# A two-block transformer in float32r: early blocks of the feed-forward corrected one by one, their products held back, and single weight blocks placed 32 bytes into their tiles

## The chip, the cores and the metric

The kernel runs on one core of a Trainium2 chip. The metric is the device time of one execution in microseconds (us), from several runs, of which the median is given. The engines are named as the profile names them: PE (TensorE, with PEld for its weight loads), DVE (VectorE), ACT (ScalarE), POOL (GpSimd) and SP (SyncE, whose queue carries the weight transfers).

## The reference

The first block has two layers (latent attention, gated linear attention, neighbourhood attention, a merge and a SwiGLU); its output of 256 tokens by 1024 goes through a second block of two layers. Each layer of the second block is

```python
x = layer_norm(ALPHA * x + 0.5 * swiglu_2(x, ffn1_w_in[l], ffn1_w_out[l]), ln_g[l, 0], ln_b[l, 0])
mix = hybrid_mixer(x, ...)
x = layer_norm(ALPHA * x + mix, ln_g[l, 1], ln_b[l, 1])
x = layer_norm(ALPHA * x + 0.5 * swiglu_2(x, ffn2_w_in[l], ffn2_w_out[l]), ln_g[l, 2], ln_b[l, 2])

def swiglu_2(x, w_in, w_out):
    h = x @ w_in
    gate, up = h[..., :D_FF], h[..., D_FF:]
    return (jax.nn.silu(gate) * up) @ w_out
```

with D = 1024 and D_FF = 2816, all in float32. The first block's layers end in the same SwiGLU behind an RMS norm.

## The kernel before

**Products.** Activations lie transposed: features on the partitions, tokens along the free dimension, so that a feature block is 128 by T. Layer 0 of the first block has T = 512, everything behind it T = 256. Each product is made of three matmuls in float32r (`mm3`, L261 to L265): weights and activations are split into a high and a low part, and high by high, high by low and low by high are added up in PSUM. A weight block of 1024 columns is loaded on SP's queue into `raw`, ACT makes `whi` of it (L250), DVE subtracts to `wlo` (L251). Both lie in tiles of 1088 columns, from column 0 or, where the product has T = 256, from column 32. There are four buffers of each; every fifth block uses a second pool, `wx`.

**Feed-forward.** `ffn_in` makes 44 blocks of 128 columns, gate and up of each of 22 pairs in turn (24 matmuls of 256 columns for a block at T = 256). `cb` takes a pair and makes one tile `u`: tanh on ACT (L1535), two operations on DVE (L1536, L1538), and a split on ACT and DVE (L495, L496). `ffn_out` makes 8 blocks of 66 matmuls over the 22 tiles `u`. A feed-forward at T = 256 stands in five places: in layer 1 of the first block (F1 in what follows), and twice in each layer of the second block (F2 and F3, F4 and F5).

**Early blocks.** PE doesn't wait for the norm ahead of a feed-forward. The blocks before `e.n` runs out (16 in these five places) are multiplied with the scaled but not yet normalized activations, `xg`, and corrected afterwards (`early_steps`, L329). The first `e.kout` of them (four, two in the first block) go through together, in banks of the PSUM pool `pa` (tag `at`, five banks); the norm's sums run through PE in between (`e.stats`). The others take a bank each of the pool `pp` (tag `mm`, three banks). Where a layer norm or a shift comes before, the moving operand has 258 columns; the two more give the terms of the correction. Weights of early blocks with 258 columns lie from column 0 of their tiles, those with 256 from column 32.

**Correction.** As soon as more than two blocks are pending, `settle` takes two, corrects both into one `fix` tile (two buffers) and hands them to `cb` at once. `fix` behind a layer norm (L1735) is a copy of two columns on DVE (`fixc`, L1738), a correction term on ACT (`lnc`, L1740), a multiplication on DVE that frees the bank (L1741), and an addition on POOL (L1742). Behind the RMS norms (L1512) it is one operation on DVE and, in layer 1 of the first block, two small ones on DVE and ACT. The normalization itself runs beside it, one of eight blocks per step (`e.apply`: L1724 on ACT, L1726 on DVE, L1728 on POOL, and a split).

**Order.** The program is traced in this order, and a planner sorts the instructions of each engine by priority and by its own estimates of time, where the data allow; each engine then runs its list strictly in order. So a setup such as `rope2` (rotary tables, masks; written behind layer 1's `ffn_in`) can be put far ahead of its place when its tiles are free.

Of the kernel before, what the change touches and what calls it, by code (L numbers as in the profile page):

```python
# [10 lines left out]
F32 = mybir.dt.float32  # L11
# [193 lines left out]
class Kern:  # L205
# [33 lines left out]

    def chunk(self, spec, T=512):  # L240


        nc = self.nc
        self.side_step()
        raw, nk, ncol, n = self.raw_chunk(spec)
        o = 32 if T == 256 else 0
        hi, lo = (self.wlast.tile([128, 1088], F32R, tag=tag, name=self.name(tag),
                                  bufs=4 if self.wlast is self.wp else 1)[:, o:o + 1024] for tag in ("whi", "wlo"))
        self.pad(self.wlast, 16)
        nc.scalar.copy(hi[:, :n], raw[:, :n])  # L250
# [3 lines left out]
    def units(self, specs, T=512):  # L254
# [11 lines left out]

    def gproj(self, spec_lists, xs, t0, t1, cb, kout=0, tail=False, early=None, ready=None, pre=()):

# [5 lines left out]
        per = 512 // T  # L274
        todo, i, got, first = list(spec_lists), 0, list(pre), bool(kout)
        if early is not None:
            i, got = yield from self.early_steps(early, todo, cb, per, T)
            first = False
            if todo or got:
                for _ in early.apply:  # L280
                    pass
                xs = early.xs
        while todo or got:
# [3 lines left out]
            while todo and len(got) < want:  # L287
                got += self.units(todo.pop(0), T)
            grp, got = got[:want], got[want:]
# [30 lines left out]
            if todo and not got and (first or AHEAD):  # L320
                got += self.units(todo.pop(0), T)
            for ps, us, i0 in banks:
# [5 lines left out]

    def early_steps(self, e, todo, cb, per, T):  # L329

# [7 lines left out]
        def matmuls(w, banks, k, pin=False):  # L338
            for wi, xi in ((0, 0), (1, 0), (0, 1)):
                for s in range(H):  # L340
                    m = nc.tensor.matmul(banks[s][:, :e.cols], lhsT=w[k][wi], rhs=e.x[k][:, xi, s, :e.cols],  # L341
                                         start=k == 0 and wi == 0 and xi == 0, stop=k == len(w) - 1 and xi == 1)
                    if pin:
                        self.tc.keep_in_program_order(m)

        def settle():
            nonlocal done
            n = min(per, len(pend))
            z = self.t(self.fixp, [128, 2, 256], F32, "fix")
            zr = z.rearrange("p a t -> p (a t)")  # L350
# [7 lines left out]
        if e.kout:  # L358
            while todo and len(got) < e.kout:
                got += self.units(todo.pop(0), Te)  # L360
            grp, got = got[:e.kout], got[e.kout:]
# [14 lines left out]
        while e.n > 0 and (got or todo):  # L376
            if not got:
                got = self.units(todo.pop(0), Te)
# [7 lines left out]
            if not got and todo and EAHEAD:  # L386
                got = self.units(todo.pop(0), Te if e.n > 0 else T)
            if len(pend) > per:
                settle()
# [1133 lines left out]
    def ffn_in(self, wname, l, xs, T, early=None, then=None):  # L1523

        nc = self.nc
        us = []
        parts = []

        def cb(ps, i, n):
            parts.extend(ps[:, a, :] for a in range(n))  # L1530
            while len(parts) >= 2:
                gate, up = parts.pop(0), parts.pop(0)
                u = self.t(self.fp, [128, 2, T], F32R, f"u{len(us)}")
                t = self.t(self.fp, [128, T], F32, "ft")
                nc.scalar.activation(t[:, :T], gate, AF.Tanh, scale=0.5)  # L1535
                nc.vector.scalar_tensor_tensor(out=t[:, :T], in0=t[:, :T], scalar=1.0, in1=gate, op0=ALU.add,  # L1536
                                               op1=ALU.mult)
                nc.vector.tensor_tensor(out=t[:, :T], in0=t[:, :T], in1=up, op=ALU.mult)  # L1538
                self.split(u[:, 0, :], u[:, 1, :], t[:, :T])
                us.append(u)  # L1540
# [45 lines left out]
    def rope2(self):  # L1586
        nc, cp = self.nc, self.cp
        with self.tc.tile_pool(name="r2", bufs=1) as rp:
            pos = self.t(rp, [128, 256], I32, "pos")
            nc.scalar.dma_start(out=pos, in_=self.ins["positions_2"].to_broadcast([128, 256]))  # L1590
            ang = self.t(rp, [128, 256], F32, "ang")
            nc.vector.tensor_copy(ang, pos)
            nc.vector.tensor_scalar(out=ang, in0=ang, scalar1=self.con("inv"), scalar2=None, op0=ALU.mult)
            n = self.t(rp, [128, 256], F32, "angn")
            big = 1.5 * 2.0 ** 23
# [49 lines left out]
    def ln_residual(self, scale, l, j, last=False):  # L1645
# [90 lines left out]
        def fix(ps, s, out):  # L1736
# [229 lines left out]
    def run(self):  # L1966
        nc, tc, ctx = self.nc, self.tc, self.ctx
        self.setup()
        with ExitStack() as hp:
            self.hp = hp  # L1970
            with self.pool("xp1", side="right") as self.xp, self.pool("wp1", 3, side="right") as self.wp:
                self.fixp = self.sp
# [94 lines left out]
```

## Time and profile before

| | |
|---|---|
| median of 3 runs | 2635.95 us (2635.83 to 2638.78) |
| the profiled execution's own time | 2630.1 us |
| its span, first to last instruction | 2628.3 us |
| mean granted TensorE clock | 0.991 |
| PE busy | 2522.5 us (96%), 17510 matmuls |
| DVE busy | 1867.1 us (71%) |
| ACT busy | 1308.2 us (50%) |
| POOL busy | 292.1 us (11%) |
| moved by DMA | 381.23 MB, mean 145 GB/s |

The profile is of one execution. Shares are averages over stages with different limits; ends of matmuls are modelled, so a busy PE isn't one at its peak, and the count of matmuls in a stretch says more than its busy time. PEclk is the granted clock as a share of 2.4 GHz. Where an engine stood idle, the view says which instruction's end let it go on.

### The profile page before, as it was taken

The numbers are of one execution on the slowest core, as the hardware profiler recorded it, in microseconds if no ns is written. First come the engines' busy times: TensorE is split into PE (matmuls) and PEld (weight loads), VectorE is DVE, ScalarE is ACT, GpSimd is POOL, SyncE is SP. The second block draws the span as 40 slices with busy tenths as digits, with TensorE's granted clock in tenths as the row PEclk, the third lists the DMA queues.
The fourth block names the chain that finished last, engine by engine and source line by source line (L and its number), as shares of the span: only waits on it lengthen the run. The fifth ranks groups of instructions, "written<-read, shape, count | busy, mean of one in ns | idle before, by whom it ended". The sixth has DMA issues, their size and how long they took to land. (4 is left out here: it accounts for less than half of the span.)

```text
span 2628.3 us, 44800 instructions
## 1 busy us (share of the span) xinstructions
PE 2522.5 (96%) x17510; PEld 2229.6 (85%) x17510; DVE 1867.1 (71%) x3318; ACT 1308.2 (50%) x2307; POOL 292.1 (11%) x368
## 2 busy tenths in 40 slices
PE   7989999999999999899999999999989999999998
PEld 4867778778777778788999999998789999977897
DVE  6677576756887865665788657667797686678965
ACT  5466633324432223566447545446475565565643
POOL 0021000110000001010020000003040040031301
PEclk9999999999999999999999999999999999999999
DMA  6332144332455543231446655553346646632563
GB/s 246 108 91 83 52 137 152 105 120 89 153 181 164 182 152 103 89 93 60 158 145 195 193 182 189 189 181 121 109 133 210 195 153 202 196 109 88 179 194 119
DMA packets 122451, 381.23 MB, mean 145 GB/s; under 512 B 25216, under 2 KB 28160, under 8 KB 122240
## 3 DMA queue, kind: packets, MB, share of 16 engines
q1 hardware_dynamic: 118784, 373.51, 45.2%
q10 hardware_dynamic: 3456, 4.86, 0.6%
q8 instruction: 138, 2.26, 0.4%
q14 instruction: 73, 0.60, 0.1%
HBM read 377.27 MB, written 1.05 MB: 144 GB/s over the span
## 5 line engine op out<-in xcount | busy, mean ns | idle before, releaser
L251 DVE TENSOR_TENSOR wlo<-raw,whi 128x1024 fp32r<-128x1024 f32 (+1 forms) x628 | 766.3, 1223 | 441.4 <-ACT whi L250 425.5
L250 ACT CAST whi<-raw 128x1024 fp32r<-128x1024 f32 (+1 forms) x628 | 637.7, 1018 | 826.2 <-PE mm L264 538.2
L263 PE MATMUL mm<-x,whi 128*128 128x256 f32 (+1 forms) x2410 | 764.8, 318 | 2.8 <-ACT whi L250 1.7
L264 PE MATMUL mm<-x,whi 128*128 128x256 f32 (+1 forms) x2410 | 760.6, 316 | 0.1
L265 PE MATMUL mm<-x,wlo 128*128 128x256 f32 (+1 forms) x2410 | 760.3, 316 | 0.1
L263 PEld LDWEIGHTS mm<-x,whi 128*128 128x128 f32 x2410 | 453.0, 188 | 48.6 <-issue 9.8
L265 PEld LDWEIGHTS mm<-x,wlo 128*128 128x128 f32 x2410 | 454.8, 189 | 33.6 <-issue 1.7
L264 PEld LDWEIGHTS mm<-x,whi 128*128 128x128 f32 x2410 | 454.9, 189 | 33.2 <-issue 1.7
L263 PE MATMUL mm<-u,whi 128*128 128x256 f32 (+1 forms) x1056 | 314.0, 297 | 0.0
L264 PE MATMUL mm<-u,whi 128*128 128x256 f32 (+1 forms) x1056 | 313.9, 297 | 0.0
L265 PE MATMUL mm<-u,wlo 128*128 128x256 f32 (+1 forms) x1056 | 313.3, 297 | 0.0
L341 PE MATMUL mm<-xg,whi 128*128 128x258 f32 (+1 forms) x1120 | 207.6, 286 | 16.4 <-DVE fixc L1738 7.2
L649 DVE SCALAR_TENSOR_TENSOR fix<-raw,csil,fix 128x512 f32<-128x512 f32 x280 | 199.0, 756 | 14.6 <-DMA raw<-in_ws_dram 14.4
L263 PEld LDWEIGHTS mm<-u,whi 128*128 128x128 f32 x1056 | 198.2, 188 | 10.7 <-issue 2.5
L265 PEld LDWEIGHTS mm<-u,wlo 128*128 128x128 f32 x1056 | 199.0, 188 | 7.2
L264 PEld LDWEIGHTS mm<-u,whi 128*128 128x128 f32 x1056 | 199.0, 188 | 6.7
L341 PEld LDWEIGHTS mm<-xg,whi 128*128 128x128 f32 x1120 | 177.1, 193 | 18.9 <-ACT whi L250 7.9
L341 PE MATMUL mm<-xg,wlo 128*128 128x258 f32 (+1 forms) x560 | 159.5, 285 | 0.0
L341 PEld LDWEIGHTS mm<-xg,wlo 128*128 128x128 f32 x560 | 108.2, 193 | 0.0
L732 ACT ACTIVATE P<-at,nmx 128x256 f32<-128x256 f32 (+1 forms) x160 | 88.5, 559 | 24.3 <-DVE nmx L727 21.5
L263 PE MATMUL mm<-whi,x 128*128 128x256 f32 x320 | 92.1, 288 | 6.9 <-ACT v L419 4.3
L725 DVE TENSOR_REDUCE mx<-at 128x1 f32<-128x512 f32 (+1 forms) x112 | 75.2, 686 | 32.0 <-PE at L954 13.0
(395 smaller groups left out, 3922.4 us busy)
## 6 DMA issues: line engine op xcount, KB each, us to landing
raw<-in_ws_dram SPq DMA_DIRECT2D x648, 512.0 KB, 3.5
raw<-in_ws_dram SPq DMA_DIRECT2D x56, 384.0 KB, 3.4
PT<-in_ws_dram SPq DMA_DIRECT2D x8, 512.0 KB, 6.8
h<-in_h_dram ACTq DMA_DIRECT2D x8, 256.0 KB, 3.8
nm<-in_na_rpb_dram SPq DMA_DIRECT2D x16, 96.0 KB, 6.6
braw<-in_na_rpb_dram SPq DMA_DIRECT2D x16, 96.0 KB, 6.5
nv<-in_h_dram ACTq DMA_DIRECT2D x4, 256.0 KB, 6.1
v<-in_h_dram ACTq DMA_DIRECT2D x4, 256.0 KB, 8.0
```

The costliest lines, as they stand in the source:

```text
L250: nc.scalar.copy(hi[:, :n], raw[:, :n])
L251: nc.vector.tensor_tensor(out=lo[:, :n], in0=raw[:, :n], in1=hi[:, :n].bitcast(F32), op=ALU.subtract)
L263: nc.tensor.matmul(out, lhsT=a[0], rhs=b[0], start=start, stop=False)
L264: nc.tensor.matmul(out, lhsT=a[0], rhs=b[1], start=False, stop=False)
L265: nc.tensor.matmul(out, lhsT=a[1], rhs=b[0], start=False, stop=stop)
L341: m = nc.tensor.matmul(banks[s][:, :e.cols], lhsT=w[k][wi], rhs=e.x[k][:, xi, s, :e.cols], start=k == 0 and wi == 0 and xi == 0, stop=k == ...
L649: nc.vector.scalar_tensor_tensor(out=acc[s], in0=w[:, j, :], scalar=x, in1=acc[s], op0=ALU.mult, op1=ALU.add)
L725: nc.vector.tensor_reduce(out=mx, in_=ps, axis=AX.X, op=ALU.max)
L732: nc.scalar.activation(P[:, i, :], ps[:, i, :], AF.Exp, bias=nm[:, i:i + 1], scale=scale, accum_out=sm[:, i:i + 1])
```

## The change

Six things change. In the feed-forward at T = 256, `settle` takes one block at a time as soon as more than one is pending, corrects it with `e.fix` into half of a `fix` tile, and puts the pair into a list `held`. A held pair is multiplied (`unit`) when its buffer is wanted again, or one by one behind the pairs of the main loop. There are four `fix` buffers in the second block (two, as before, in the first). Early blocks with an odd number take their bank from `pa` in place of `pp`. The addition in `fix` behind a layer norm goes from POOL to DVE, in the mixers too. And the first weight chunk of blocks 6, 18 and 23 of `ffn_in` and of block 0 of `ffn_out` lies from column 8 of its tiles (32 bytes), if it is loaded for T = 256. To make room, `rope2`'s tables use `ft` tiles of the feed-forward's pool instead of a pool of their own, and a pad of 32 bytes goes from the pool `yp`, into which `ls` comes.

```diff
-    def chunk(self, spec, T=512):
+    def chunk(self, spec, T=512, place=None):
...
-        o = 32 if T == 256 else 0
+        o = place if place is not None else 32 if T == 256 else 0
...
-        parts = [(self.chunk(s, T), len(s[2])) for s in specs]
+        parts = [(self.chunk(s, T, None if i else place), len(s[2])) for i, s in enumerate(specs)]
...
+        def load(to=T):
+            spec = todo.pop(0)
+            return self.units(spec, to, places.get(total - len(todo) - 1) if to == 256 else None)
...
+        dst = getattr(e, "dst", None)
+
         def settle():
             nonlocal done
+            if dst is not None:
+                e.fix(pend.pop(0)[0], 0, dst(done))
+                done += 1
+                return
             n = min(per, len(pend))
-            z = self.t(self.fixp, [128, 2, 256], F32, "fix")
+            z = self.fixtile()
...
-            banks = [self.t(self.pp, [128, 512], F32, "mm") for _ in range(H)]
+            pool, tag = (self.pa, "at") if dst is not None and i % 2 else (self.pp, "mm")
+            banks = [self.t(pool, [128, 512], F32, tag) for _ in range(H)]
...
-            if len(pend) > per:
+            while len(pend) > (per if dst is None else 1):
                 settle()
...
+    def fixtile(self):
+        return self.fixp.tile([128, 2, 256], F32, tag="fix", name=self.name("fix"), bufs=self.nfix)
...
+        us = [None] * NJ
+        parts, held = [], []
+
+        def unit(j, gate, up):
+            u = us[j] = self.t(self.fp, [128, 2, T], F32R, f"u{j}")
+            t = self.t(self.fp, [128, T], F32, "ft")
+            nc.scalar.activation(t[:, :T], gate, AF.Tanh, scale=0.5)
+            nc.vector.scalar_tensor_tensor(out=t[:, :T], in0=t[:, :T], scalar=1.0, in1=gate, op0=ALU.add,
+                                           op1=ALU.mult)
+            nc.vector.tensor_tensor(out=t[:, :T], in0=t[:, :T], in1=up, op=ALU.mult)
+            self.split(u[:, 0, :], u[:, 1, :], t[:, :T])
+
+        def release():
+            j, z = held.pop(0)
+            unit(j, z[:, 0, :], z[:, 1, :])
+
+        def dst(b):
+
+            if b % 2 == 0:
+                while len(held) >= self.nfix:
+                    release()
+                held.append((b // 2, self.fixtile()))
+            return held[-1][1][:, b % 2, :]
 
         def cb(ps, i, n):
-            parts.extend(ps[:, a, :] for a in range(n))
+            parts.extend((i + a, ps[:, a, :]) for a in range(n))
             while len(parts) >= 2:
...
+                (j, gate), (_, up) = parts.pop(0), parts.pop(0)
+                unit(j // 2, gate, up)
+            if held:
+                release()
+
+        if early is not None and T == 256:
+            early.dst = dst
...
-                           early=early)
+                           early=early, places={b: 8 for b in (6, 18, 23)})
...
-        self.proj([_colblock(wname, l, NJ, _rng(o * 128)) for o in range(8)], us, 0, T, cb, tail=True)
+        self.proj([_colblock(wname, l, NJ, _rng(o * 128)) for o in range(8)], us, 0, T, cb, tail=True,
+                  places={0: 8})
...
-        self.pad(self.yp, 8)
...
-        self.fixp = self.yp
+        self.fixp, self.nfix = self.yp, 4
...
-            pos = self.t(rp, [128, 256], I32, "pos")
+            pos = self.t(self.fp, [128, 256], F32, "ft").bitcast(I32)
...
-            ls = self.t(rp, [128, 2, 2], F32, "ls")
+            ls = self.t(self.yp, [128, 2, 2], F32, "ls")
...
-            nc.gpsimd.tensor_tensor(out=out, in0=out, in1=ck, op=ALU.add)
+            nc.vector.tensor_tensor(out=out, in0=out, in1=ck, op=ALU.add)
```

## Rows read from the trace of the kernel before

**Rows 1.** The page: busy time, share of the span, instructions of each engine.

```profile
span 2628.3 us, 44800 instructions
PE 2522.5 (96%) x17510; PEld 2229.6 (85%) x17510; DVE 1867.1 (71%) x3318; ACT 1308.2 (50%) x2307; POOL 292.1 (11%) x368
```

**Rows 2.** Stage table (PE, PEld, DVE, ACT, POOL busy; PEclk; DMA; GB/s): F3, F4, F5, F1, F2.

```profile
1929.00:1969.00 40.00, 34.71 (x276) 34.19 (x275) 39.27 (x68) 28.96 (x53) 23.07 (x22) 0.96 0.41 139
2118.00:2159.00 41.00, 35.96 (x288) 35.60 (x288) 37.91 (x67) 29.16 (x53) 20.97 (x21) 0.96 0.48 154
2439.00:2478.00 39.00, 32.96 (x272) 32.25 (x271) 37.15 (x68) 28.48 (x53) 20.33 (x21) 1.00 0.42 135
1424.00:1457.00 33.00, 33.00 (x281) 33.00 (x280) 30.73 (x71) 23.85 (x44) 0.00 (x0) 1.00 0.63 198
1613.00:1644.00 31.00, 31.00 (x266) 31.00 (x265) 27.67 (x50) 17.67 (x28) 1.86 (x4) 1.00 0.62 202
```

**Rows 3.** Waits of PE (us in total, times, longest): F3; F4; F5.

```profile
PE mm L341 <- DVE fixc L1738: 3.5, 2, 1.7
...
PE mm L341 <- DVE fix L1741: 5.0, 2, 2.9
...
PE mm L341 <- DVE fixc L1738: 3.8, 2, 2.0
```

**Rows 4.** Chain of waits through F3's early stretch, 1929 to 1969 us, shares.

```profile
by line: DVE wlo L251 23.9%; DVE x L496 11.9%; DMA raw<-in_ws_dram 10.7%; issue 10.7%; DVE fix L1741 7.7%; DVE ft L1536 7.4%; DVE ft L1538 6.4%; POOL fix L1742 5.2%; DVE u L496 4.4%; POOL h L1728 4.3%; DVE lnt L1726 4.2%; DVE fixc L1738 1.6
```

**Rows 5.** Table by stage, PE alone, 70 us of the main loops of F1 to F4.

```profile
1460.00:1530.00 70.00, 70.00 (x596) 1.00 0.59 187
1650.00:1720.00 70.00, 70.00 (x596) 1.00 0.57 185
1970.00:2040.00 70.00, 69.95 (x617) 1.00 0.67 209
2162.00:2232.00 70.00, 70.00 (x620) 1.00 0.64 198
```

**Rows 6.** The same, 50 us of the output blocks (`ffn_out`) of F1 and F5.

```profile
1540.00:1590.00 50.00, 50.00 (x427) 1.00 0.61 192
...
2560.00:2610.00 50.00, 50.00 (x444) 1.00 0.49 145
```

**Rows 7.** Groups of DVE, 1926 to 1969 us (busy us, mean ns | idle).

```profile
L251 DVE TENSOR_TENSOR wlo<-raw,whi 128x1024 fp32r<-128x1024 f32 x12 | 17.6, 1474 | 0.4 <-ACT whi L250 0.4
L1536 DVE SCALAR_TENSOR_TENSOR ft<-ft,fix 128x256 f32<-128x256 f32 x7 | 5.6, 798 | 0.0
...
L1741 DVE TENSOR_TENSOR fix<-mm,rr 128x256 f32<-128x256 f32 x10 | 4.1, 411 | 0.0
```

**Rows 8.** Groups of POOL in the same window.

```profile
L1742 POOL TENSOR_TENSOR fix<-fix,lnc 128x256 f32<-128x256 f32 x14 | 16.6, 1196 | 26.0 <-ACT lnc L1740 14.0 <-DVE fix L1741 8.9 <-DVE fixc L1738 2.0
L1728 POOL TENSOR_TENSOR h<-lnt,lnc 128x256 f32<-128x256 f32 x8 | 7.5, 939 | 2.3 <-ACT lnc L1724 1.3 <-DVE lnt L1726 0.9
```

**Rows 9.** Groups of DVE in F1's early stretch, 1424 to 1457 us.

```profile
L251 DVE TENSOR_TENSOR wlo<-raw,whi 128x1024 fp32r<-128x1024 f32 x13 | 15.9, 1220 | 2.0 <-ACT whi L250 2.0
...
L1536 DVE SCALAR_TENSOR_TENSOR ft<-ft,fix 128x256 f32<-128x256 f32 x7 | 2.9, 419 | 0.0
```

**Rows 10.** Table by stage, DVE alone, first 22 us of F5's main loop.

```profile
2480.00:2502.00 22.00, 18.50 (x27) 1.00 0.79 247
```

**Rows 11.** Timeline, F3: DVE's first corrections; ACT ahead of them.

```profile
1927.21 0.75 DVE L1741 TENSOR_TENSOR fix<-at,rr 128x256 f32<-128x256 f32 x2
...
1926.38 2.00 ACT L250 CAST whi<-raw 128x1024 fp32r<-128x1024 f32 x2 [2.15 <-DMA raw<-in_ws_dram]
1928.29 1.08 ACT L1740 ACTIVATE lnc<-rr,fixc 128x256 f32<-128x256 f32 x2
```

**Rows 12.** A wait of PE in the first mixer of the second block.

```profile
PE at L1754 <- ACT rraw L1752: 2.7, 2, 2.4
```

**Rows 13.** Timeline of ACT: a step of `rope2`.

```profile
1389.94 0.42 ACT L1642 ACTIVATE sin<-ang 128x256 f32<-128x256 f32 x1
```

More of the change, by code (lines that the diff above doesn't have):

```diff
@@ L252, in chunk, with units @@
         return (hi[:, :n].rearrange("p (k c) -> p k c", k=nk), lo[:, :n].rearrange("p (k c) -> p k c", k=nk))
-    def units(self, specs, T=512):
-        parts = [(self.chunk(s, T), len(s[2])) for s in specs]
+    def units(self, specs, T=512, place=None):
+        parts = [(self.chunk(s, T, None if i else place), len(s[2])) for i, s in enumerate(specs)]
         ncb = len(specs[0][3]) // 128
@@ L265, in mm3, with gproj @@
         nc.tensor.matmul(out, lhsT=a[1], rhs=b[0], start=False, stop=stop)
-    def gproj(self, spec_lists, xs, t0, t1, cb, kout=0, tail=False, early=None, ready=None, pre=()):
+    def gproj(self, spec_lists, xs, t0, t1, cb, kout=0, tail=False, early=None, ready=None, pre=(), places=None):
         nc = self.nc
@@ L275, in gproj @@
         todo, i, got, first = list(spec_lists), 0, list(pre), bool(kout)
+        total, places = len(todo), places or {}
+        def load(to=T):
+            spec = todo.pop(0)
+            return self.units(spec, to, places.get(total - len(todo) - 1) if to == 256 else None)
         if early is not None:
-            i, got = yield from self.early_steps(early, todo, cb, per, T)
+            i, got = yield from self.early_steps(early, todo, cb, per, T, load)
             first = False
@@ L287, in gproj @@
             while todo and len(got) < want:
-                got += self.units(todo.pop(0), T)
+                got += load()
             grp, got = got[:want], got[want:]
@@ L320, in gproj @@
             if todo and not got and (first or AHEAD):
-                got += self.units(todo.pop(0), T)
+                got += load()
             for ps, us, i0 in banks:
@@ L327, in gproj, with early_steps @@
             yield
-    def early_steps(self, e, todo, cb, per, T):
+    def early_steps(self, e, todo, cb, per, T, load):
         nc = self.nc
@@ L359, in early_steps @@
             while todo and len(got) < e.kout:
-                got += self.units(todo.pop(0), Te)
+                got += load(Te)
             grp, got = got[:e.kout], got[e.kout:]
@@ L377, in early_steps @@
             if not got:
-                got = self.units(todo.pop(0), Te)
+                got = load(Te)
             w = got.pop(0)
-            banks = [self.t(self.pp, [128, 512], F32, "mm") for _ in range(H)]
+            pool, tag = (self.pa, "at") if dst is not None and i % 2 else (self.pp, "mm")
+            banks = [self.t(pool, [128, 512], F32, tag) for _ in range(H)]
             for k in range(len(w)):
@@ L386, in early_steps @@
             if not got and todo and EAHEAD:
-                got = self.units(todo.pop(0), Te if e.n > 0 else T)
-            if len(pend) > per:
+                got = load(Te if e.n > 0 else T)
+            while len(pend) > (per if dst is None else 1):
                 settle()
@@ L1525, in ffn_in @@
         nc = self.nc
-        us = []
-        parts = []
+        us = [None] * NJ
[17 more added lines that the diff above has]
+            return held[-1][1][:, b % 2, :]
         def cb(ps, i, n):
-            parts.extend(ps[:, a, :] for a in range(n))
+            parts.extend((i + a, ps[:, a, :]) for a in range(n))
             while len(parts) >= 2:
[L1532 to L1540, printed above, removed]
+                (j, gate), (_, up) = parts.pop(0), parts.pop(0)
[4 more added lines that the diff above has]
+            early.dst = dst
         cols = [_rng(a + j * 128) for j in range(NJ) for a in (0, DFF)]
         steps = self.gproj([_colblock(wname, l, KB, c) for c in cols], xs, 0, T, cb, kout=2 if T == 512 else 4,
-                           early=early)
+                           early=early, places={b: 8 for b in (6, 18, 23)})
         if then is not None:
@@ L1587, in rope2 @@
         nc, cp = self.nc, self.cp
-        with self.tc.tile_pool(name="r2", bufs=1) as rp:
-            pos = self.t(rp, [128, 256], I32, "pos")
+        if True:
+            pos = self.t(self.fp, [128, 256], F32, "ft").bitcast(I32)
             nc.scalar.dma_start(out=pos, in_=self.ins["positions_2"].to_broadcast([128, 256]))
-            ang = self.t(rp, [128, 256], F32, "ang")
+            ang = self.t(self.fp, [128, 256], F32, "ft")
             nc.vector.tensor_copy(ang, pos)
             nc.vector.tensor_scalar(out=ang, in0=ang, scalar1=self.con("inv"), scalar2=None, op0=ALU.mult)
-            n = self.t(rp, [128, 256], F32, "angn")
+            n = self.t(self.fp, [128, 256], F32, "ft")
             big = 1.5 * 2.0 ** 23
@@ L1971, in run @@
             with self.pool("xp1", side="right") as self.xp, self.pool("wp1", 3, side="right") as self.wp:
-                self.fixp = self.sp
+                self.fixp, self.nfix = self.sp, 2
                 first = self.layer(0, 512, self.first_norm, lambda: self.load_h(hp.enter_context(self.pool("hp"))))
```

## The prediction

> **What bounds the kernel now.** I read the page first: the span is 2628.3 us, PE is busy for 2522.5 us of it, DVE for 1867.1, ACT for 1308.2, POOL for 292.1 [rows 1]. So the time can fall only where PE stands idle or runs slower than it can, and I looked for such places in the stages that the diff touches. These are five passes of `ffn_in` and `ffn_out` at T=256; I call them F1 (first block, layer 1), F2 and F3 (second block, layer 0), F4 and F5 (second block, layer 1). Each begins with an early stretch of 16 blocks (columns of 128, 24 matmuls each), whose banks are corrected afterwards, and goes on with 28 blocks and the 8 output blocks.
>
> Next I took the table by stage over the early stretches [rows 2]. In F3, F4 and F5 PE is busy for 34.71 of 40, 35.96 of 41 and 32.96 of 39 us: 5.3, 5.0 and 6.0 us idle. In F1 and F2 it is idle for nothing. The granted clock is 0.96 in the windows of F3 and F4, that is, it lay at 1.2 instead of 2.4 GHz for a part after PE had stood: 4% of 40 and 41 us, 1.6 us each. The rest ran at 1.00.
>
> Who ends the idle time says the view of waits [rows 3]: nearly all of it is PE at L341 waiting for `fix` or `fixc` on DVE, the readers that give a bank back. The chain of F3's stretch shows DVE at each step, `wlo` alone with 23.9% [rows 4]. DVE is busy for 39.27 of 40 us there [rows 2]: in this stretch it is the bound, not PE.
>
> Last I took the rate of PE where nothing stalls it. Over 70 us of the main loop PE starts 596 matmuls in F1 and F2, but 617 and 620 in F3 and F4, with the same tiles and the granted clock at 1.00 [rows 5]: 70/593 = 118.0 ns against 70/617 = 113.4 ns from start to start (three at the edges taken off). The output blocks show the same two levels, 427 in 50 us of F1, 444 of F5 [rows 6], and each pass keeps the level of its main loop. A level, once taken, holds over a whole stage, and F2's early stretch of 256 columns lies on the slow one too (266 in 31 us [rows 2]). The early stretches of 258 columns run at about 118.7 ns in F1 [rows 2], yet the main loops behind them go to 113.4 in three cases of four.
>
> **The change part by part.** The time before is the median 2635.95 us; the profiled run took 2630.1, its span 2628.3. I make the sum as a difference within the span and take it off the median.
>
> 1. The add of `fix` from POOL to DVE. In F3's window of 43 us, POOL runs 14 of these (1196 ns each, 16.6 us) beside 8 of L1728 (7.5 us) [rows 8]. DVE's own operations are stretched beside them: `wlo` takes 1474 ns, the first operation on `ft` 798 [rows 7], in F1's stretch, where POOL is idle, 1220 and 419 [rows 9]. At such prices [rows 7, 9], with 0.45 for `lnt` and 0.15 for `fixc`, F3's DVE work would be 12 x 1.22 + 14 x 0.41 + 12 x 0.15 + 8 x 0.45 + 8 x 0.42 + 19 x 0.42 + 0.4 = 37.6 us (`wlo`, `fix`, `fixc`, `lnt`, `x`, units, `rr`); the eleven groups of that window, from `wlo` with 17.6, sum to 47.3. So 9.7 us are stretch; by POOL's time 69% of it, 6.7 us, goes with the 14 adds, and 3.0 stays with L1728. The adds cost DVE 14 x 0.41 = 5.7 us.
>
> 2. Gates and ups kept. Four pairs stay in `fix` tiles until the main loop, so that the window holds 4 units, not 19/3 = 6.3: 2.3 x 3 x 0.42 = 2.9 us less. Sum for DVE: 37.6 + 5.7 - 2.9 = 40.4; adjoining operations overlap by some 0.08 us (in F1's stretch the twelve groups, from `wlo` with 15.9, sum to 36.5, while the engine is busy for 30.73 with 71 instructions [rows 2, 9]), for 80 of them 6.4. 40.4 - 6.4 + 3.0 = 37.0 us of DVE. Without idle time and low clock PE would need 43 - 5.3 - 1.6 = 36.1. DVE and PE then match, and with five more banks in turn PE can run ahead of DVE by several blocks, now by three. I leave 1.5 us of idle time in each of F3 to F5: 16.3 - 4.5 = 11.8 us gained, and the low clock with it, 2 x 1.6 = 3.2 us. Together 15.0; the bounds are 0 and 19.5, and if DVE has to wait, below zero (second rival). F1 and F2 have no stall to lose; DVE at 30.73 of 33 us leaves them cover. The four held units come to the main loop at 4 x 3 x 0.42 = 5.0 us of DVE over eight blocks. It is busy 18.50 of 22 us there in F5 [rows 10], so 23.5 less twelve overlaps of 0.08, 22.5, would fill it: hidden if its `wlo` come ahead, as in F1's 93%; if not, 1.5 us per pass, 7.5 at most.
>
> 3. More banks: the odd early blocks take `at` banks. Five are there, four hold the first blocks and one the statistics, so block 5 needs the first one back. In F3 its `fix` starts at 1927.21 [rows 11], one block of 2.85 us and more before block 5 could start. I cost it at nothing, and up to 1 us per pass if that order is lost.
>
> 4. The 32 bytes. The diff shifts one weight block at three places of F1, F3, F4 and F5 and at four of F2 (block 6 is loaded for 256 columns there): 16 blocks of 24 matmuls. Taken as a thing of its own it can cost 16 x 24 x 4.6 ns = 1.8 us if each such block falls to the slow level. But it also disturbs the rhythm of loads and matmuls. F1 and F2 from block 18 on have 1152 + 1584 matmuls at the slow level; at the fast one they gain 2736 x 4.6 ns = 12.6 us. No shift of this kind is in the trace; the bounds are -12.6 us and, if F3 to F5 fall to the slow level, +3 x 1152 x 4.6 ns = +15.9. The nearest rows are the steps from 258 to 256 columns, where the operands move as well and no stall lies between: three of four went to the fast level. So I take the gain, less 1 us for the blocks themselves: 11.6 us.
>
> The Trainium skill speaks against this term. "SBUF — State Buffer", section "SBUF: two separate sides", says that on the engine side only the port pair that VectorE and GpSimd share causes contention, and that PE never waits there. By it the start of a weight tile is nothing to PE, and the sum would be without the 11.6 us. This case's trace has two levels for one shape [rows 5], which the rule doesn't explain.
>
> 5. The rest. The mixers get the add on DVE alone (their settling stays in twos): PE waits for `rraw` there for 2.7 us in the first of the two [rows 12], behind `fix`. I take 1 us of gain for both, bounds -3 and +3. The tables of `rope2` move: `sin` is made at 1389.94 us [rows 13], before F1 begins; with `ft` tiles of F1 it can't start before F1's last units, and falls into `ffn_out`. A dozen operations of DVE and ACT of some 0.4 us stand there beside a PE that is never starved [rows 6]: nothing; at most 1.5 us, if they come ahead of a `whi`.
>
> Sum: -15.0 - 11.6 - 1.0 = -27.6 us; 2635.95 - 27.6 = 2608.
>
> **The rivals.**
> - The shift does nothing to the levels: 2635.95 - 16.0 = 2620. For it: both levels live through 28 blocks and many tile buffers without a change [rows 5, 6]; against it, the step that came with 256 columns. It is what the Trainium skill's page "SBUF — State Buffer" would give.
> - DVE waits for ACT. This ends on the other side. The moved add stands in DVE's order behind `lnc` of ACT (1.08 us for two), and that behind two `whi` of 1.0 us each [rows 11]. On POOL such a wait held nobody's `wlo`; on DVE it holds the next `wlo` and the next bank. With one `whi` in front of each add, DVE loses about 1.0 us 14 times per stretch: 14 - 5.3 = +9 per pass, +27 in all with the mixers' adds not counted: 2663 with the levels as they are, 2651 with them mended. It decides from about 0.4 us of wait per add, where the gain of part 1 and 2 is gone. Against it: `lnc` can run while DVE does the multiplication or a `wlo` of another block.
> - The shift breaks the fast level. F1 and F2 gain, F3 to F5 lose as much or more: -16.0 - 11.6 + 15.9 = -11.7, 2624.
> - The stalls stay since the work of DVE only changes its kind: -3 instead of -15, and with the levels mended 2621, else 2633.
>
> **How the numbers follow.** The forecast has 0.50; the shift without effect 0.20, the fast level broken 0.13, stalls that stay 0.09 (half of it with the levels mended), DVE behind ACT 0.08. About 0.2%, 5.3 us, is what a measurement can tell from no change. Faster holds 0.50 + 0.20 + 0.12 + 0.05 = 0.87, within 0.2% 0.06, slower 0.07. The range of 8 in 10 goes from 2600 (19.5 + 12.6 + 3 gained would be 2601) to 2628, where the cases around 2620 and 2624 still lie inside; the forecast's own is 2601 to 2615.
>
> **What would show it.** The windows of F3 to F5: PE idle under 2 us each, the clock at 1.00, POOL with L1728 alone, `wlo` near 1.3 us. F1 and F2: 617 and more matmuls in 70 us from block 18 on, with the step at block 18, 23 or the first output block; F3 to F5 still so. Wrong it would be if DVE shows idle time before the adds ended by `lnc`, or if the counts stay at 596.

## The result, and the profile after

The changed kernel takes 2599.26 us (median of 4 runs, 2597.44 to 2601.78). The kernel before took 2637.36 us in the runs beside it (4 runs, 2635.83 to 2644.45). The ratio is 0.9855, 95% interval 0.9838 to 0.9872: 38 us faster. That is 0.7 us below the low end of my range. The profiled execution took 2597.44 us with a span of 2595.7, 32.6 us less than the span of before [rows 1]. The page's busy line:

```profile
span 2595.7 us, 44682 instructions
PE 2508.1 (97%) x17510; PEld 2217.0 (85%) x17510; DVE 1866.0 (72%) x3382; ACT 1307.7 (50%) x2307; POOL 224.2 (9%) x303
```

PE is busy for 14.4 us less with the same matmuls; the other 18.2 us are idle time that went. DVE has the 64 adds more, POOL 65 instructions less.

To place the gain I took the length of each stage, from its first matmul to the next stage's first; the borders are good to 0.2 us. "Third" and "again" are further profiled executions of the two kernels, told of below.

| stage, us | before | after | change | before, third | after, again |
|---|---|---|---|---|---|
| start to F1 | 1408.7 | 1406.5 | -2.2 | 1410.7 | 1409.5 |
| F1 early, main, output | 47.8, 79.3, 62.3 | 46.9, 76.5, 60.1 | -0.9, -2.8, -2.2 | 47.9, 79.3, 62.3 | 46.9, 76.7, 60.1 |
| F2 early, main, output | 46.0, 79.3, 62.4 | 44.9, 76.4, 60.1 | -1.1, -2.9, -2.3 | 46.0, 79.3, 62.4 | 44.9, 76.4, 60.1 |
| first mixer | 125.3 | 122.3 | -3.0 | 125.3 | 122.6 |
| F3 early, main, output | 57.7, 76.7, 60.0 | 52.6, 76.5, 60.1 | -5.1, -0.2, +0.1 | 57.6, 79.5, 62.4 | 52.5, 76.5, 60.1 |
| F4 early, main, output | 54.3, 76.3, 60.0 | 47.2, 76.5, 60.1 | -7.1, +0.2, +0.1 | 54.3, 76.3, 60.0 | 47.2, 76.5, 60.1 |
| second mixer | 125.2 | 122.3 | -2.9 | 125.0 | 122.6 |
| F5 early, main, output | 57.2, 76.3, 60.0 | 56.6, 76.5, 60.1 | -0.6, +0.2, +0.1 | 57.1, 76.3, 60.0 | 56.5, 76.5, 60.1 |

The table by stage, in the order of [rows 2] (F3, F4, F5, F1, F2; columns as there):

```profile
1911.00:1946.00 35.00, 34.31 (x281) 33.90 (x280) 34.49 (x75) 28.11 (x49) 8.91 (x12) 1.00 0.47 150
2095.50:2129.50 34.00, 34.00 (x289) 34.00 (x288) 31.76 (x68) 26.31 (x45) 9.77 (x9) 1.00 0.48 158
2406.00:2445.00 39.00, 35.24 (x278) 34.62 (x277) 35.38 (x81) 29.31 (x52) 9.91 (x8) 0.96 0.46 147
1421.00:1453.00 32.00, 32.00 (x272) 32.00 (x271) 30.38 (x70) 24.37 (x42) 0.00 (x0) 1.00 0.62 196
1604.00:1634.00 30.00, 30.00 (x265) 30.00 (x264) 24.47 (x43) 14.54 (x20) 0.90 (x4) 1.00 0.64 202
```

PE's idle time went from 5.3 to 0.7 us in F3 and from 5.0 to nothing in F4. In F5 3.8 us are left, and the granted clock is 0.96 there, where it was 1.00 before. F2 starts 265 matmuls in 30 us; before it took 31 us for 266.

PE alone (busy, PEclk, DMA share, GB/s), 70 us of the main loops of F1 to F5 and 50 us of the output blocks of F1 and F5, which answer to [rows 5, 6]:

```profile
1457.00:1527.00 70.00, 70.00 (x618) 1.00 0.60 194
1638.00:1708.00 70.00, 70.00 (x619) 1.00 0.62 192
1950.00:2020.00 70.00, 70.00 (x619) 1.00 0.64 209
2133.00:2203.00 70.00, 70.00 (x619) 1.00 0.67 210
2449.00:2519.00 70.00, 70.00 (x619) 1.00 0.64 204
1535.00:1585.00 50.00, 50.00 (x443) 1.00 0.64 195
2527.00:2577.00 50.00, 50.00 (x444) 1.00 0.46 146
```

All five passes run at the fast level; 596 and 427 are gone.

The groups of DVE, and then of POOL, in F3's early stretch (1903 to 1946 us), against [rows 7, 8]:

```profile
L251 DVE TENSOR_TENSOR wlo<-raw,whi 128x1024 fp32r<-128x1024 f32 x14 | 18.0, 1288 | 0.0
L1778 DVE TENSOR_TENSOR fix<-fix,lnc 128x256 f32<-128x256 f32 x14 | 7.4, 526 | 0.1
...
L1550 DVE SCALAR_TENSOR_TENSOR ft<-ft,fix 128x256 f32<-128x256 f32 x4 | 1.7, 416 | 0.0
```

```profile
L1764 POOL TENSOR_TENSOR h<-lnt,lnc 128x256 f32<-128x256 f32 x8 | 7.0, 873 | 30.5 <-ACT lnc L1760 29.5 <-DVE fixc L1774 1.0
```

As forecast, POOL is left with its other add alone, `wlo` falls from 1474 to 1288 ns, and the first operation on `ft` from 798 to 416. The moved add takes 526 ns here, for which I had set 410.

What PE waits for in F5's early stretch, against the last line of [rows 3]:

```profile
PE at L348 <- DVE wlo L251: 2.8, 2, 2.1
PE at L348 <- DVE xg L1706: 1.5, 2, 1.1
PE mm L348 <- DVE wlo L251: 1.0, 1, 1.0
```

The wait for `fixc` is gone, and so is one of before that I had passed over when I put nearly all of the idle time down to `fix` and `fixc`:

```profile
PE mm L341 <- ACT x L495: 2.3, 2, 1.7
```

PE now waits for weights (the wait for `xg` was 1.4 us before). The chain of waits there (start and length in us, what) shows who makes them late:

```profile
2428.18 0.50 ACT lnc L1760
2428.75 1.62 POOL h L1764
2430.40 0.42 ACT x L509
2430.84 0.43 DVE x L510
...
2433.45 1.68 DVE wlo L251
2435.18 4.53 PE at L348 x23
```

The other add of the normalization is still on POOL and takes 1.62 us. ACT's split stands in its list behind it, DVE's half of the split (L510) behind that, with 1.1 us of idle time ahead of it, and `wlo` further down the list ends 2.1 us too late for PE. The 23 matmuls behind it take 4.53 us: PE had stood, and the clock then lay at 1.2 instead of 2.4 GHz for most of the next 3.8 us (PE busy, granted clock, DMA share, GB/s):

```profile
2435.60:2439.40 3.80, 3.80 (x21) 0.55 0.73 204
```

### The profile page after: what moved, and what is told of

The parts are those of the page before. It is cut to its first block, busy times and chain, and to the rows that moved or that the text cites. A ratio compares the mean times of both kernels' runs of the same rounds, so it can differ in the third digit from the quotient of the medians.

```text
span 2595.7 us, 44682 instructions
## 1 busy us (share of the span) xinstructions
PE 2508.1 (97%) x17510; PEld 2217.0 (85%) x17510; DVE 1866.0 (72%) x3382; ACT 1307.7 (50%) x2307; POOL 224.2 (9%) x303
## 4 chain that ended last, share of the span: by engine, by line
PE 79%; DVE 10%; ACT 4%; issue 4%; DMA 2%; POOL 1%; SPq 0%; ACTq 0%; POOLq 0%; DVEq 0%
PE mm L263 21%; PE mm L264 21%; PE mm L265 20%; PE at L348 4%; PE mm L348 2%; DVE wlo L251 2%; PE at L770 1%; PE at L783 1%; DMA raw<-in_ws_dram 1%; PE at L971 1%; ACT whi L250 1%; DVE mx L742 1%; PE at L673 1%; ACT P L749 1%; DVE fix L666 1%
## 5 line engine op out<-in xcount | busy, mean ns | idle before, releaser
L263 PEld LDWEIGHTS mm<-x,whi 128*128 128x128 f32 x2410 | 452.6, 188 | 48.7 <-issue 10.9
L666 DVE SCALAR_TENSOR_TENSOR fix<-raw,csil,fix 128x512 f32<-128x512 f32 x280 | 198.8, 754 | 13.1 <-DMA raw<-in_ws_dram 12.8
L348 PE MATMUL at<-xg,whi 128*128 128x258 f32 (+1 forms) x912 | 173.9, 285 | 3.3 <-DVE xg L1706 3.1
L348 PEld LDWEIGHTS at<-xg,whi 128*128 128x128 f32 x912 | 144.7, 191 | 4.9 <-DVE xg L1706 4.5
L348 PE MATMUL at<-xg,wlo 128*128 128x258 f32 (+1 forms) x456 | 129.6, 285 | 3.6 <-DVE wlo L251 3.4
L348 PE MATMUL mm<-xg,whi 128*128 128x258 f32 (+1 forms) x624 | 117.8, 282 | 0.0
L348 PEld LDWEIGHTS mm<-xg,whi 128*128 128x128 f32 x624 | 98.8, 189 | 0.8 <-issue 0.7
```

Of the source, the lines that this page charges most:

```text
L263: nc.tensor.matmul(out, lhsT=a[0], rhs=b[0], start=start, stop=False)
L666: nc.vector.scalar_tensor_tensor(out=acc[s], in0=w[:, j, :], scalar=x, in1=acc[s], op0=ALU.mult, op1=ALU.add)
```

## The experiments

My theories: the shift breaks the slow level of F1 and F2; the held products and the add off POOL empty the stalls of F3 to F5. The rivals stand in the prediction; others came from what each run left.

**The shift alone**, put into the kernel before (together with the lines of the change that hand `places` through to `chunk`):

```diff
-                           early=early)
+                           early=early, places={b: 8 for b in (6, 18, 23)})
...
-        self.proj([_colblock(wname, l, NJ, _rng(o * 128)) for o in range(8)], us, 0, T, cb, tail=True)
+        self.proj([_colblock(wname, l, NJ, _rng(o * 128)) for o in range(8)], us, 0, T, cb, tail=True,
+                  places={0: 8})
```

> The kernel before with nothing but the 32-byte shift of blocks 6, 18, 23 and of output block 0. Theory (a shifted block breaks the slow level and leaves the fast one alone): F1 and F2 go to 113.2 ns from block 18 (F1) and block 6 (F2) on, shifted blocks run at 116.6 ns, F3 to F5 keep 113.2; the five stages of F1 and F2 lose 2.3 + 2.3 + 1.0 + 2.9 + 2.3 us, about 11 us in all, span near 2617, ratio 0.996. Rival (the level is set by how a pass is entered, and the changed early stretch did it): F1 and F2 stay at 118 ns, span near 2629, ratio 1.000.

Measured: 2622.95 us (10 runs, 2617.03 to 2624.46) against 2635.73, ratio 0.9955 (0.9939 to 0.9970). Its early stretches of F3 to F5 stay at 57.7, 52.7 and 57.5 us. PE in the main loops of F1 and F2, and in 12.3 us before and behind F2's shifted block 6 (1608.9 to 1611.7 us):

```profile
1459.00:1529.00 70.00, 70.00 (x618) 1.00 0.59 193
1640.00:1710.00 70.00, 70.00 (x619) 1.00 0.60 192
```

```profile
1597.00:1609.30 12.30, 12.30 (x107) 1.00 0.45 143
1613.00:1625.30 12.30, 12.30 (x111) 1.00 0.58 196
```

Four matmuls more in the same time, with the clock at 1.00 on both sides: the level changes at the shifted block. In F1 the 24 matmuls of blocks 16 and 17 take 2828 and 2826 ns, those of the shifted block 18 2799, those of block 19 and the next ones 2720. So a shifted block has a rate of its own, 116.6 ns, and leaves the fast level behind it. F5 was entered slow in this execution (blocks 16 and 17 take 2828 and 2826 ns) and went the same way behind its block 18, so it didn't keep the fast level, as I had expected, but came to it. My theory holds for the rest, with the step where I had put it.

**The changed kernel without the shift:**

```diff
-                           early=early, places={b: 8 for b in (6, 18, 23)})
+                           early=early, places={})
...
-                  places={0: 8})
+                  places={})
```

> The changed kernel without the shift. Theory: F2's early stretch falls to 118 ns behind the norm's sums as it does with the shift, but stays there through F2's main loop and output blocks: about 200 + 1200 matmuls at 4.6 ns more, +6.5 us; F1 is entered at the fast level and keeps it; every pass that happens to be entered slow stays slow to its end, 5.5 us each. Span 2602 to 2613. Rival (entry alone): F2 returns to the fast level by itself at its main loop; span within 2 us of 2596.

Measured: 2609.9 us (6 runs, 2606.9 to 2618.47), ratio 0.9918 (0.9890 to 0.9947): 10.6 us more than the changed kernel. F1 and F2 are slow throughout, F1 too, which I had expected to be entered fast:

```profile
1459.00:1529.00 70.00, 70.00 (x596) 1.00 0.59 186
1646.00:1716.00 70.00, 70.00 (x597) 1.00 0.57 186
```

So nothing else in the change brought F1 and F2 to the fast level here. Over all profiled runs the output blocks, which keep the level of their pass, were slow in 12 of 25 passes without the shift (the kernel before three times, this run, the add alone) and in none of 35 with the single shifted blocks.

**The add alone**, moved to DVE in the kernel before:

```diff
-            nc.gpsimd.tensor_tensor(out=out, in0=out, in1=ck, op=ALU.add)
+            nc.vector.tensor_tensor(out=out, in0=out, in1=ck, op=ALU.add)
```

> The kernel before with the add of the correction on DVE instead of POOL, nothing else. Theory (the add's place is what the two mixers gained): mixers 122.5 us instead of 125.4 each, -5.8; early stretches of F3 to F5 gain the stretch of DVE's operations less the adds, 1 to 2 us each: -9 to -12 us in all, span 2616 to 2620. Rival (the mixers gained by four correction buffers instead of two): mixers stay at 125.4, span 2623 to 2626. Second rival (DVE waits behind ACT): early stretches get longer, span above 2630.

Measured: 2628.18 us (10 runs, 2622.14 to 2634.33), ratio 0.9972 (0.9950 to 0.9995). The early stretches gain 0.8, 2.4 and 0.8 us only, and F4's may not be the add's (52.7 us in another execution of the kernel before, 51.9 here); the mixers gain 2.9 and 2.7, all that they gain in the changed kernel. In F3 PE still waits for the banks:

```profile
PE mm L341 <- DVE fixc L1738: 3.1, 2, 1.7
PE mm L341 <- DVE fix L1741: 1.2, 1, 1.2
PE mm L341 <- DVE wlo L251: 1.2, 1, 1.2
```

while `wlo` is down to 1217 ns. So taking POOL's stretch off DVE doesn't empty the stalls. F5's main loop shows one thing more. It was entered slow (block 16 takes 2826 ns); in block 17 PE waits for `wlo` for 1.2 us; from block 18 on each takes 2720. There is no shift in this kernel: a stall of PE, too, can end the slow level.

**The changed kernel with the add back on POOL** (the same line, reversed):

> The changed kernel with the add back on POOL. Theory: both mixers go back to 125.4 us (+5.8), and F3's and F4's early stretches lose most of their gain, since DVE is stretched again beside POOL: +3 to +5 each, 12 to 16 us in all, span 2608 to 2612. Rival (holding the products back is enough by itself): early stretches within 1.5 us of the changed kernel's, only the mixers lose, span near 2602.

Measured: 2602.54 us (4 runs, 2600.56 to 2604.21), ratio 0.9885 (0.9854 to 0.9917). The mixers lose 2.5 us each. But F3's early stretch takes 51.7 us (52.6 in the changed kernel), F4's 48.0 (47.2), F5's 51.7 (56.6). DVE's `wlo` of F5 (2406 to 2447 us):

```profile
L251 DVE TENSOR_TENSOR wlo<-raw,whi 128x1024 fp32r<-128x1024 f32 x13 | 18.2, 1415 | 0.1
```

```profile
PE at L348 <- DVE wlo L251: 1.1, 1, 1.1
```

With `wlo` at 1415 ns, stretched as before, PE has one wait of 1.1 us left there (the second fence, 2414 to 2447 us). That part of my theory falls, and so does the rival in F5, which is 4.9 us shorter than in the changed kernel. The main loops behind, of F3 to F5, pay for a part: 0.6, 1.1 and 1.0 us more.

**The changed kernel without holding** (and so with corrections in pairs, and the banks of before):

```diff
-        if early is not None and T == 256:
+        if False:
             early.dst = dst
```

> The changed kernel with settling in twos, products at once and early banks from the old pool again; add on DVE, shift and four correction buffers stay. Theory (holding back and more banks are what emptied the stalls of F3 and F4): early stretches of F3, F4, F5 at 56.9, 51.9, 56.4 us as with the add alone, against 52.6, 47.2, 56.6 now; levels and mixers as in the changed kernel; span near 2605. Rival (four buffers and the add are enough): F3 and F4 within 1.5 us of 52.6 and 47.2, span near 2596.

Measured: 2610.36 us (4 runs, 2607.3 to 2612.41), ratio 0.9901 (0.9871 to 0.9930). F3 to F5's early stretches go back to 56.0, 50.6 and 55.5 us, and F5's main loop takes 80.6: in block 17 PE waits once for `wlo`, for 1.8 us, and behind that, from 2457 to 2461 us, the granted clock is 0.66, so that this block takes 6.4 us. Block 16 had run at the fast level. The shifted block 18, right behind that stretch, takes 2800 ns and this once leaves the slow level behind it: blocks 19 to 22 take 2826 to 2828 ns each, until the shifted block 23 ends that. The waits of F3 are those of the kernel before again:

```profile
PE mm L348 <- DVE fixc L1774: 3.1, 2, 1.7
PE mm L348 <- DVE fix L1777: 1.2, 1, 1.2
```

Holding and the banks that go with it take the waits away; the two weren't separated, nor from settling one block at a time.

**Every block shifted**, in the changed kernel:

```diff
-                           early=early, places={b: 8 for b in (6, 18, 23)})
+                           early=early, places={b: 8 for b in range(44)})
...
-                  places={0: 8})
+                  places={b: 8 for b in range(8)})
```

> The changed kernel with the first chunk of every block of the feed-forwards that is loaded for T = 256 at column 8. Theory (the shift changes the matmul's rate only while the shifted weights are loaded, and leaves the fast level behind): main loops all at 116.6 ns from the first shifted block, 28 x 24 x 116.6 = 78.4 us each instead of 76.5, output blocks 24 x 116.6 + 42 x 113.2 each, 60.7 instead of 60.1; +1.9 + 0.6 in five passes and some 0.8 in F2's early stretch, about +13 us, span near 2609. Rival (the shift itself is the faster place, and one would want it everywhere): main loops at or below 76.5, span at or below 2596.

Measured: 2616.41 us (4 runs, 2615.53 to 2617.92), ratio 0.9925 (0.9896 to 0.9954). The main loops of F1, F3 and F4:

```profile
1462.00:1532.00 70.00, 70.00 (x603) 1.00 0.59 187
...
1960.00:2030.00 70.00, 70.00 (x602) 1.00 0.67 209
2147.00:2217.00 70.00, 70.00 (x596) 1.00 0.65 202
```

603 in 70 us is 116.7 ns, the rate of single shifted blocks; F4 and F5 stay at 118.0 though each of their blocks is shifted. So 8 columns isn't a faster place than 32. What goes with the fast level is a change from one place to the other. The output blocks of this run, where 24 matmuls of each 66 are shifted, show it: F4, slow up to there, is fast behind its first 24. But one way back isn't always enough: F5 goes on slow through the 42 behind its first 24, and is fast only behind the next shifted ones.

**The add on POOL in the feed-forwards, on DVE in the mixers:**

```diff
-            nc.vector.tensor_tensor(out=out, in0=out, in1=ck, op=ALU.add)
+            (nc.gpsimd if hasattr(e, "dst") else nc.vector).tensor_tensor(out=out, in0=out, in1=ck, op=ALU.add)
```

> The changed kernel with the correction's add on POOL in the feed-forwards (early blocks that are held back) and on DVE in the mixers. Theory (with products held back nobody waits soon for the add, so that in the feed-forwards POOL is the better place, and in the mixers DVE): F5's early stretch 51.7 us instead of 56.6, F3's 51.7 instead of 52.6, F4's 48.0 instead of 47.2, main loops about 0.7 us longer each, mixers 122.4; span 2592 to 2594. Rival (F5's 51.7 with the add on POOL was the clock's luck): F5 at 55 to 57, span 2596 to 2598.

Measured: 2598.43 us (6 runs, 2595.86 to 2605.29), ratio 0.9862 (0.9835 to 0.9889): no different from the changed kernel. F5's early stretch comes down to 52.7 us, but the main loops of F3 to F5 take 0.6 to 1.1 us more, and with them goes part of the gain.

**Both adds on DVE** (L1764 too), in the changed kernel:

```diff
-                nc.gpsimd.tensor_tensor(out=self.x2[k], in0=t1, in1=ck, op=ALU.add)
+                nc.vector.tensor_tensor(out=self.x2[k], in0=t1, in1=ck, op=ALU.add)
```

> The changed kernel with the addition of the normalized block (L1764, eight of 128x256 per layer norm) on DVE too, so that POOL runs nothing beside the early stretches of F3 to F5. Theory (what the last runs left: DVE is the bound of F5's early stretch, and moving an add to it costs more than the POOL stretch that it removes): 8 x 0.42 = 3.4 us of DVE work more per stretch against some 3 us of stretch less, so the five early stretches stay within 1 us of the changed kernel's (46.9, 44.9, 52.6, 47.2, 56.6) and the time within 3 us of 2599. Rival (what costs DVE its time is POOL at work beside it, however few its operations): wlo falls from 1.35 us to 1.22 in F3 and F5, F5's stretch falls by 3 to 5 us, the time to 2592 or less. Third (DVE's order decides): L1764 in DVE's list comes ahead of wlo and of fix, and F3 and F5 lengthen by 3 us each, 2605 or more.

Measured: 2591.55 us (4 runs, 2590.66 to 2592.39), ratio 0.9824 (0.9797 to 0.9852) against 2637.05: faster than both kernels, by 9.5 us than the changed kernel's one run beside it (2601.07), by 7.7 than its median of four above. My theory was wrong, and the rival's numbers came true. F3 and F5 (2405 to 2439.5 us), and DVE's groups of F5:

```profile
1912.00:1946.80 34.80, 34.41 (x287) 34.00 (x287) 34.43 (x85) 28.79 (x50) 1.94 (x4) 1.00 0.45 156
...
2405.00:2439.50 34.50, 34.42 (x284) 34.17 (x283) 34.39 (x86) 28.13 (x49) 0.00 (x0) 1.00 0.46 158
```

```profile
L251 DVE TENSOR_TENSOR wlo<-raw,whi 128x1024 fp32r<-128x1024 f32 x11 | 13.3, 1213 | 0.0
L1778 DVE TENSOR_TENSOR fix<-fix,lnc 128x256 f32<-128x256 f32 x14 | 5.8, 421 | 0.0
```

F5's early stretch takes 51.7 us, and DVE has no idle time and no POOL beside it. But the rival's reason, POOL at work beside DVE, isn't shown by this: with the add on POOL `wlo` is slowest (1415 ns), and F5 takes 51.7 us as well. DVE waits there for ACT's split and for POOL (2.1 and 3.2 us) longer than in the changed kernel (2.1 and 0.6), but has no adds to make. It seems to take both, adds on DVE and waits, to make PE late. That is argued: as the planner sorts the lists of each kernel anew, their order may have a part in it. The mixers gain 1.2 us more each, to 121.1: the wait for `rraw` of [rows 12] was 2.7 us, is 1.3 in the changed kernel, and is 0.2 here.

**The kernel before, twice more**, unchanged:

> The kernel before once more, for another profiled execution. Theory (its executions differ by the level that each pass is entered at, which nothing mends): some of the passes F1 to F5 have another level than in the first profile (slow F1 and F2, fast F3 to F5), and the span differs by about 5.5 us for each such pass. Rival (the levels are fixed by the program, the executions differ by transfers at the start or by stalls): the same levels pass by pass, with the difference elsewhere.

> The kernel before, unchanged, for a third profiled execution of it. Theory (the passes' rates are drawn anew in each execution, and the shift takes the draw away): F1 to F5 each have main loops of either 76.3 to 76.7 us or 79.3 us and output blocks of 60.0 or 62.3, nothing between, and which passes are slow may differ from the two executions seen (F1, F2; F1, F2, F5). Each slow pass more than these two adds 5.3 us to the span of 2628, each less takes 5.3 off. Rival (the second execution's slow F5 was an accident of one run, and F1 and F2 are slow by their place in the program): F1 and F2 slow, F3 to F5 fast, span 2628 within 2.

Measured: 2636.07 and 2637.16 us, where the first profiled execution took 2630.1. The one has F5 slow as well as F1 and F2, the other F3. PE in the main loop of F5 in the former (the first fence), of F3 and F5 in the latter:

```profile
2482.00:2552.00 70.00, 70.00 (x597) 1.00 0.64 202
```

```profile
1974.00:2044.00 70.00, 70.00 (x594) 1.00 0.61 201
...
2488.00:2558.00 70.00, 70.00 (x620) 1.00 0.64 209
```

The same program, another pass at the slow level: main loop 79.3 or 79.5 instead of 76.3 or 76.7, output blocks 62.3 or 62.4 instead of 60.0. A pass's level isn't a property of its place. F3 of the latter wasn't even entered slow: block 16 takes 2742 ns, block 17 3159, with 350 ns from one start to the next at one place, and the blocks from there on 2826 or 2827 each. In the two other executions F3 has such a break, too (329 and 326 ns), and stays fast. F1 and F2 were slow in all three. For F2 the changed kernel shows where it is taken each time: its first early block still runs at 113 ns a matmul, the next ones, behind the four matmuls of the norm's sums, at 118, until block 6 ends that.

**The changed kernel again:**

> The changed kernel, unchanged, for a second profiled execution. Theory (the single shifted blocks bring every pass to the fast rate, whichever it was entered at): all five main loops 76.3 to 77.0 us, all output blocks 60.1, whatever the early stretches before them; the early stretch of F5 again some 56 us, since it is DVE's list that sets it; span 2592 to 2600. Rival (that all five were fast was luck of the one profiled run): at least one main loop at 79.3 and one output stretch at 62.3.

Measured: 2601.07 us, span 2599.2. All five main loops took 76.4 to 76.7 us, all outputs 60.1; F5's early stretch took 56.5. Both statements held. F1 shows the step in this execution: blocks 16 and 17 take 2827 ns each, the shifted block 18 2798, block 19 2720.

## Why the prediction was wrong in size

The direction was right, and no rival came true as a whole. The sum of -27.6 us stands against -32.6 between the first two spans and -38.1 between the medians. Of the 10.5 us between sum and medians, 5.4 lie in the base of the sum (the two profiled executions lay 7.3 and 1.8 us below the medians of their runs) and 4.9 in the mixers; the way up to F1 and F1's early stretch, which the sum had at nothing, gave 3.1; the early stretches of F3 to F5 gave 2.2 less than put, the levels 0.8 less.

- **The levels (part 4: -11.6).** In the first pair of traces the five places where a level changed (F1 main and output, F2 early, main and output) give -2.8 - 2.2 - 1.1 - 2.9 - 2.3 = -11.3 us. Place and size were as put, and the shift alone and its absence confirm that the shift ends the slow level; that it does so by disturbing a rhythm is not shown. I had counted F2 from its first block (1584 matmuls), though its first shifted one is block 6: from there it is 1440, and the gain 11.9 - 1 = 10.9. The runs give -11.3 and +0.5 for the shifted blocks of F3 to F5, together -10.8. Not as put is that a level holds over a whole stage: in three main loops it changed at a stall or a break of PE. In the first trace of the changed kernel F1 was fast from block 16 on, before any shifted block, which is not the shift's merit; in the second it was entered slow and went to the fast level behind block 18.
- **The base of the sum ("a difference within the span and take it off the median").** This step failed. The first profiled execution lay 5.9 us below the median, and I carried its two slow passes over to all. The two other executions, at the median, have three. From "before, third" to "after, again" the span falls by 36.2 us, of it 16.4 by the levels: a third slow pass gives 5.3 more than the first pair's 11.3, and F1, entered slow, 0.2 less. The shift seems to take away a part of what differs between executions: in one session ten runs of the shift alone spread over 7.4 us, ten of the add alone over 12.2, the 21 of before over 26. Whether each execution of before at the median has a third slow pass, three traces don't say; the runs of the shift alone have their median 5.9 us above their own profiled one, and what differs there isn't seen.
- **The mixers (part 5: -1.0, bounds -3 and +3).** The second step that failed, and the term most off: -3.0 and -2.9, together 5.9, beyond my bound. The add alone does it. I had priced the one wait that I saw, 2.7 us in one mixer; the second mixer has the same of 2.4 us, eight adds of 1.1 to 1.2 us on POOL run in each, and the first also lost a stretch of half clock behind its stall (0.66 in a window of 5 us of the kernel before, 1.00 after). The two waits fall to 1.3 us each, which makes 2.5 of the 5.9; where the rest lies isn't placed.
- **The early stretches (parts 1 to 3: -15.0).** They gave 5.1 + 7.1 + 0.6 = 12.8 us. The split by cause was wrong. The lengths of F3, F4 and F5 in five kernels:

| early stretch, us | F3 | F4 | F5 |
|---|---|---|---|
| add on POOL, no holding (before) | 57.7 | 54.3 | 57.2 |
| add on DVE, no holding (the add alone) | 56.9 | 51.9 | 56.4 |
| add on POOL, held | 51.7 | 48.0 | 51.7 |
| add on DVE, held (the change) | 52.6 | 47.2 | 56.6 |
| both adds on DVE, held | 51.1 | 47.2 | 51.7 |

  I made the stalls a matter of DVE's amount of work: 9.7 us of stretch, most of it to go with the add. But how full DVE is doesn't decide: with both adds on DVE it is busy for 34.43 of 34.8 us in F3, and PE stands for 0.4 us; with the add alone it is busy for 37.28 of 39.5, and PE stands for 5.5. The runs fit the order of DVE's list instead: a bank came free only behind the operations on `ft` of the pairs before it, which stand in the chain of [rows 4]. Holding those back, with the banks that go with it, gives 5 to 6 us without the add (F4's stretch of before is 52.7 in one more of its executions); since it also takes work out of the stretch and adds banks, the order as the cause is argued and not shown. The add on DVE then changes the stretches by -0.8 to +4.9 us, against the sign that I had given it in F3 and F5, and saves the 0.6 to 1.1 us of each main loop. In F5 it stands in one list with waits for the add left on POOL, which is what the rival "DVE waits for ACT" had in mind: DVE idles for ACT's split twice, for 1.1 us each, and not 14 times. My 1.5 us of idle time left in each was 0.7, 0.0 and 3.8.
- **More banks and the tables of `rope2` (nothing).** The output blocks of F1 take 60.1 us with the tables moved and with the shift alone, so the tables cost nothing there. The way up to F1 lies between 1405 and 1412 us over all kernels; its -2.2 can't be put down to the change. The 0.9 us of F1's early stretch lie in its first two blocks, which run beside the norm's sums; those behind take 2845 to 2851 ns each in both kernels. They stay without the shift and without holding (46.9 and 47.0 us), so neither makes them.

On `wlo`, which has two inputs in SBUF, the Trainium skill's page "SBUF — State Buffer", section "SBUF: two separate sides", gives a reason: VectorE and GpSimd share a port pair that one holds for a whole instruction. The traces agree in the direction, the lock itself none shows: in F5 `wlo` takes 1415 ns beside some 20 adds on POOL, 1298 beside eight, 1213 beside none, while `fix` from PSUM takes 410 to 419 in all three. The same section's sentence that PE never waits on anyone doesn't account for the two rates, between which a weight block's place in its tile moved PE (118 to 113 ns); whether PE waits for anything there no run shows.

## What to carry to other kernels

When one shape shows two rates in a profile, take several executions of the same kernel before pricing it: one profile holds one draw, and the median of the runs another. A stall "behind DVE" can be the amount of its work or the order of its list; what gives a bank back should stand ahead of work that nobody waits for yet. Where a chain passes between engines, try moving it whole: here, with the pairs held, one of the two adds moved cost F5's stretch 5 us, both moved cost it nothing.

## What the runs showed of the hardware that I had not expected

With the granted clock at 1.00 and the same tiles, 24 matmuls of 256 columns take 2720, 2799 or 2828 ns. Which of the first and the last it is, is taken at some entry, differs from one execution to the next, and held for a thousand matmuls and more where nothing came between. Where only single blocks are shifted, one whose weights lie 32 bytes into their tile ended the slow level 14 times of 14 where no stall lay right before or in it, and once, right behind a stall, it didn't; shifting all of them leaves 603 or 596 matmuls in 70 us. A stall, or a break of some 0.2 us between two matmuls, can change the level either way: from 2826 to 2720 ns in F5 of the add alone, from 2742 to 2827 in F3 of a run of the kernel before, from 2740 to 2828 in F5 without holding. Why is not known, and other distances than 32 bytes weren't tried.
